# An encoder trunk on one core: wide products in the input projection, squares moved, two edits at the ends

## The chip, the core and the metric

The kernel runs on one core of a Trainium2 chip. The metric is the device time of one execution in microseconds, as the median of several runs. The engines are named as in the profile: PE (matrix products; PEld is its weight load), DVE (VectorE), ACT (ScalarE), POOL (GpSimd) and SP (it issues DMAs). Each has a queue of its own and works it off in order.

## The reference, cut to what matters

Two layers over 256 positions and 2048 channels, all in float32:

```python
hn = _rmsnorm(h, norm_g[i])
u = hn @ w_in[i]
a_val, a_glu, a_z, q, k, v, b_z = jnp.split(u, offs, axis=-1)
ya = _conformer_conv(a_val, a_glu, ...) * jax.nn.silu(a_z)   # GLU, 31-tap depthwise conv, LayerNorm, SiLU
yb = _window_attention(q, k, v, bias_band, sink[i]) * jax.nn.silu(b_z)
h = h + jnp.concatenate([ya, yb], axis=-1) @ w_out[i]
e = _rmsnorm(p[i] @ w_pe[i], pe_g[i])
h = h + e * jax.nn.sigmoid(h @ w_pg[i])
```

After the second layer a last RMSNorm is applied. The input projection has 5632 columns: 1024 each for the convolution's value, GLU and gate and for the query and the attention gate, 256 each for keys and values.

## The kernel before, in words

Everything is held transposed: 128 channels on the partitions, 256 positions along the row. To keep float32 accuracy on PE, each operand is split into a high and a low part (`hi`, rounded to PE's format, and `lo`, the rest), and a product of a weight tile w with an operand x is the sum of w_hi x_hi, w_hi x_lo and w_lo x_hi. `mm3` (L384) issues it in one of two ways. With a 256-column output it is three instructions of 256 columns into the same half of a PSUM bank (L391 to L393). With an output of three dimensions, a whole bank, it is one instruction of 512 columns, w_hi times x_hi and x_lo side by side (L388), and one of 256 columns, w_lo times x_hi, into the second half (L389). The two halves of the bank then have to be added: `merge` (L395) lets ACT copy the second half to SBUF and DVE add the first half to it. Before, only the gate of the embedding (the product with `w_pg`, tile `g`) is done in the wide way.

The weights stream in through 312 half tiles of 128 x 1024, 8 products each, in the order of `HALVES`: per layer 4 for the embedding's projection (`w_pe`), 32 for value and GLU (tile `ag`, 8 channel tiles), 4 for keys, 4 for values, 32 for attention gate and query in turn (tiles `zb` and `q`, pairs of tiles), 16 for the convolution gate (`za`), then 32 each for the output projection (`o`) and the embedding's gate (`g`). Working off one half is a step. At the start of step h the halves up to h + 4 are split (`get`, `ahead`, `split`, L159): ACT casts the high part (L163), DVE subtracts it from the weight (L166). There are five buffers of split weights. After each step `pump` (L198) is called once; it moves all side work on, which is written as generators: the generators in `side`, each by one `yield`, and then convolution taps from `conv_q`, at a rate per step that `RATES` sets by the place in the layer: one rate to the 56th half, one to the 80th, one behind. A convolution tile is one ACT instruction (L550) and 30 DVE taps (L557); two tiles run in turn. PE, DVE and ACT keep the order of the program as written, so this pump is the schedule.

The places that the change touches:

- `glu` (L564): after a value/GLU tile ACT takes the sigmoid of the GLU half from PSUM (L566) and DVE multiplies the value half with it (L567); then the tile joins the convolution queue. Value and GLU share one bank.
- The loop over `zb` and `q` (L668): `pair` fills one bank with two tiles of 256 columns. ACT takes the SiLU of the gate pair from PSUM (L671). Of the query pair ACT writes a negated, scaled high part (L677) and DVE the rest (L678); two generators of attention are queued, whose scores (tile `sc`, L626) come two steps later.
- The loop over `za` (L684) does the same as for the gate pair (L690).
- `embed` (L517): the generator for the RMSNorm of the embedding. Its squares are taken during the value/GLU stage, two tiles at a time, the square on ACT and the running sum on POOL (`square_acc`, L371); then a fold on DVE, a column of sums on PE, a power on POOL, and the row of factors. The factors are applied in the gate stage (L536), when `state["enorm"]` is set.
- The start (L274): x is loaded by four DMAs from ACT's queue, p and the first weights from SP's queue. PE begins with four products of zeros (L256).
- The end (L838): the last RMSNorm. A column of sums, power on POOL, a diagonal on DVE (L350), a product that spreads it over the partitions (tile `rfb`, L356). Ahead of that product PE is given 14 idle products (L842), each of two passes.

Of the kernel before, what the change touches and what calls it, by code (L numbers as in the profile page):

```python
# [10 lines left out]
F32 = mybir.dt.float32  # L11
F32R = mybir.dt.float32r
AF = mybir.ActivationFunctionType
# [4 lines left out]
P = 128  # L18
D = 2048
S = 256  # L20
# [105 lines left out]
def trunk_kernel(ctx: ExitStack, tc: tile.TileContext, xT, pT, wst, par, gain, relb, sinkp, onehot, out):  # L126
    nc = tc.nc
# [7 lines left out]
    wk = ctx.enter_context(tc.tile_pool(name="wk", bufs=2))  # L135
# [10 lines left out]
    def bank(name):  # L146
        return ps.tile([P, 2, S], F32, tag="ps", name=name)

    LD, LS = 3, NSPL - 1
    state = {"raw": -1, "spl": 3, "credit": 0.0}  # L150
# [42 lines left out]

    conv_q, side = [], []

    RATES = (3.3, 2.6, 3.3)

    def pump(taps=None):  # L198
        taps = RATES[(Cursor.h % NHALF > 4 + 32 + 8 + 12) + (Cursor.h % NHALF > 4 + 32 + 8 + 32 + 4)] if taps is None else taps
        state["credit"] += taps  # L200
        if ORD:
            sides()
        while state["credit"] >= 1 and conv_q:
            g = conv_q.pop(0)
            try:
                next(g)
                state["credit"] -= 1
                conv_q.insert(1, g)
            except StopIteration:
                pass  # L210
        if not conv_q:
            state["credit"] = 0.0
        if not ORD:
            sides()

    def sides():
        for g in list(side):
            try:
                next(g)
            except StopIteration:  # L220
                side.remove(g)
# [10 lines left out]
    def wait(n):  # L232
        for _ in range(n):
            yield
# [17 lines left out]
    zeros = wk.tile([P, S], F32, name="zeros", tag="sq", bufs=3)  # L252
# [10 lines left out]
    def load_half(c, x, n=1):  # L263

        if x == 0:
            raws[c] = wraw.tile([P, 2, HALF], F32, tag="raw", name=f"raw{c}")
        w = HALF // n
        for i in range(n):
            nc.sync.dma_start(raws[c][:, x, i * w:(i + 1) * w], wst[c, :, x * HALF + i * w:x * HALF + (i + 1) * w])

    def load_x(k):
        nc.scalar.dma_start(h[k // 8][:, k % 8:k % 8 + 4, :], xT[:, k:k + 4, :])

    h = halves(bigt("x"))  # L274
    pf = load_p(0)
    load_half(0, 0, 2)
    for k in range(0, KT, 4):
        load_x(k)
    load_half(0, 1)
# [38 lines left out]
    def bias_prep():  # L318
        nc.vector.tensor_scalar(nsink, sinkt, -1.0, None, ALU.mult)
        b = bank("fps").rearrange("p a b -> p (a b)")  # L320
        nc.tensor.matmul(b[0:NQ, 0:NREL], relt, oh, start=True, stop=True)
        fs = wk.tile([NQ, NREL], F32, name="fs", tag="sq", bufs=3)
        nc.vector.tensor_copy(fs, b[0:NQ, 0:NREL])
        nc.gpsimd.dma_start(fscr[:, 0:NREL], fs)
# [46 lines left out]
    def square_acc(acc, src, first, eng=None):  # L371

        if first:
            nc.scalar.activation(acc, src, AF.Square)
            return
        sq = wk.tile([P, 2, S], F32, name="sq", tag="sq", bufs=3)
        nc.scalar.activation(sq, src, AF.Square)
        (eng or nc.gpsimd).tensor_add(acc, acc, sq)
# [5 lines left out]
    def mm3(o, w, x, start, stop):  # L384
# [7 lines left out]
        nc.tensor.matmul(o, w[:, 0], x[:, 1], start=False, stop=False, skip_group_check=True)  # L392
        nc.tensor.matmul(o, w[:, 1], x[:, 0], start=False, stop=stop, skip_group_check=True)  # L393

    def merge(bs):  # L395

        t = wk.tile([P, 2, S], F32, name="hl", tag="ptt")[:, 0:len(bs), :]
        for x, b in enumerate(bs):
            nc.scalar.copy(t[:, x, :], b[:, 1, :])
            nc.vector.tensor_add(t[:, x, :], b[:, 0, :], t[:, x, :])  # L400
        return t

    class Cursor:
# [2 lines left out]
    def step(o, X, start, stop):  # L406

        steps([o], X, [start], stop)

    def steps(os, X, starts, stop):  # L410

        parts = []
        for _ in os:
            name, _, k0, nk = HALVES[Cursor.h % NHALF]
            parts.append(get(Cursor.h).rearrange("p t (k c) -> p t k c", k=nk))
            Cursor.h += 1
        for kk in range(nk):
            k = k0 + kk
            for o, w, start in zip(os, parts, starts):
                mm3(o, w[:, :, kk, :], X[k // 8][:, :, k % 8, :], start and kk == 0, stop and kk == nk - 1)  # L420
        for _ in os:
            pump()

    def pair(X, name):
        b = bank(name)
        for x in range(2):
            step(b[:, x, :], X, x == 0, False)
            step(b[:, x, :], X, False, True)
        return b

    def wide(X, name):

        b = bank(name)
        step(b, X, True, False)
        step(b, X, False, True)
        return b
# [6 lines left out]
    hacc = wk.tile([P, 2, S], F32, name="hacc", tag="hacc")  # L443
    for l in range(DEPTH):

        e = halves(bigt(f"e{l}"))
        eacc = wk.tile([P, 2, S], F32, name="eacc", tag="hacc")

        hg = []
        rbs, subs = [], []  # L450
# [21 lines left out]
        for q in range(4):  # L472
            n = Cursor.h
# [5 lines left out]
            for jj in range(0, 4, 2):  # L479
                j = 4 * q + jj  # L480
                b = bank("e")
# [32 lines left out]
        ahead(Cursor.h + 3)  # L514
        hsrc = xT if l == 0 else hscr

        def embed(l=l, eacc=eacc, e=e):  # L517

            if l == 0:
                yield from wait(8)  # L520
                bias_prep()
            for j in range(0, KT, 2):
                yield from wait(2)
                square_acc(eacc, e[j // 8][:, j % 8:j % 8 + 2, :], j == 0)
            yield from wait(6)
            es = fold(eacc)
            yield from wait(3)
            dg = rstd_col([es], D, f"re{l}")
            yield from wait(2)
            eb = rstd_row(dg, f"re{l}", "reb")  # L530
            yield from wait(50)
            while not state["enorm"]:
                yield
            for j in range(KT):
                d = e[j // 8][:, j % 8, :]
                nc.vector.scalar_tensor_tensor(d, d, pcol(l, PO_PE + j), eb, ALU.mult, ALU.mult)  # L536
                yield

        state["enorm"] = False
        engen = embed()  # L540
        side.append(engen)


        a, acc = halves(bigt(f"ac{l}"))
# [18 lines left out]

        def glu(t, b):  # L564
            u = wk.tile([P, S], F32, name=f"u{l}_{t}", tag="sg")
            nc.scalar.activation(u, b[:, 1, :], AF.Sigmoid)  # L566
            nc.vector.tensor_mul(a[:, t, :], b[:, 0, :], u)  # L567
            conv_q.append(conv(t))

        for ts in FIRST_TILES:  # L570
            bs = [bank(f"ag{l}_{t}") for t in ts]
            for n in range(2):
                for t, b in zip(ts, bs):
                    if len(ts) > 1:
                        steps([b[:, 0, :], b[:, 1, :]], hg, [n == 0, False], n == 1)
                        if n == 0:
                            operands(8 + 4 * t, 2)
                            subs.pop(0)()
                    else:
                        for x in range(2):  # L580
                            step(b[:, x, :], hg, n == 0 and x == 0, n == 1)
                    if n == 1:
                        glu(t, b)


        b = pair(hg, f"k{l}")
# [9 lines left out]
        for q in range(4):  # L596
            n = Cursor.h
# [12 lines left out]
        zb, za = halves(bigt(f"z{l}"))  # L610
# [56 lines left out]

        for i in range(0, 8, 2):  # L668

            b = pair(hg, f"zb{l}_{i}")  # L670
            nc.scalar.activation(zb[:, i:i + 2, :], b, AF.Silu)  # L671
            b = pair(hg, f"q{l}_{i}")

            qq = wk.tile([P, 2, 2, S], F32R, name="qq", tag="qq")
            for hh in range(2):
                r, o = rows_of[hh], rows_of[1 - hh]
                nc.scalar.mul(qq[r, :, hh, :], b[r], -(HD ** -0.5))  # L677
                nc.vector.scalar_tensor_tensor(qq[o, :, hh, :], b[r], -(HD ** -0.5), qq[r, :, hh, :].bitcast(F32),  # L678
                                               ALU.mult, ALU.subtract)
            for x in range(2):  # L680
                side.append(attention(i + x, qq[:, x], 4 * x))


        for t in range(0, NCT, 2):  # L684
            b = pair(hg, f"za{l}_{t}")
            if t == NCT - 2:
                finish(l)
                yb = bigt(f"yb{l}", F32R)
                nc.scalar.copy(yb[:, 0, 0:2, :], zb[:, 0:2, :])
            nc.scalar.activation(za[:, t:t + 2, :], b, AF.Silu)  # L690

        ya = bigt(f"ya{l}", F32R)

# [47 lines left out]
            step(ob[j // 2][:, j % 2, :], Y, j % 2 == 0, False)  # L741
        while lgen in side:
            pump(0)
        h1 = []

        def load_h(j):
# [27 lines left out]
        for j in range(NB_FIRST, KT, 2):  # L774
            b = bank(f"o{l}_{j}")
# [6 lines left out]
        hacc = wk.tile([P, 2, S], F32, name="hacc", tag="hacc")  # L782
# [43 lines left out]
        for j in range(KT - 2, KT):  # L826
            if last and j == KT - 1:
                b = bank(f"g{l}_{j}")[:, 0:1, :]
# [9 lines left out]
    dg = rstd_col(hparts, D, "rf")  # L838

    wb = bank("warm2")  # L840
    for _ in range(14):
        nc.tensor.matmul(wb[:, 0, 0:P], ones, ident, start=True, stop=True)  # L842
    rb = rstd_row(dg, "rf", copy=False)
    rbs = wk.tile([P, S], F32, name="rfrb", tag="rb", bufs=1)
# [86 lines left out]
```

## Time and profile before

| | |
|---|---|
| runs, median (lowest to highest) | 987.34 us (987.12 to 987.56) |
| profiled execution, its own time | 988.23 us |
| its span, first to last instruction | 986.5 us |
| mean granted PE clock | 0.995 |
| DVE, weight splits (L166) | 372.8 us busy, 306 instructions |
| ACT, weight casts (L163) | 316.2 us busy, 308 instructions |
| DVE, convolution taps (L557) | 480 instructions |

In rows of a timeline stand the start, the busy time, the engine, the line and operation, output and inputs by the program's names with partitions x elements, and in brackets the idle time of the engine before it with what ended it. Rows of busy time by stretch give the stretch, its length, the busy time and number of instructions of each engine asked for, the granted PE clock, and the share and rate of the DMAs. Rows of waits give who waited for whom: the total in us, how often, and the longest.

### The profile page before, as it was taken

What the parts mean: (1) busy time and instruction counts of PE and PEld (TensorE: products, weight loads), DVE (VectorE), ACT (ScalarE), POOL (GpSimd) and SP (SyncE); (2) the same over time, 40 slices, a digit from 0 to 9 for tenths busy, and PEclk for the clock granted to TensorE, in tenths of its full rate; (3) what the DMA queues carried; (4) which work ended last, traced back from release to release, by engine and by line L of the source; (5) the groups of instructions that cost most, each with busy time, mean ns of one, the idle gap of its engine ahead of it and who ended that gap; (6) DMA issues with size and microseconds to landing.
All of it is one profiled execution on the core that took longest, in us unless ns stands there. A gap on an engine that the chain in (4) does not pass through costs nothing.

```text
span 986.5 us, 18195 instructions
## 1 busy us (share of the span) xinstructions
PE 970.2 (98%) x7460; PEld 929.8 (94%) x7460; DVE 774.8 (79%) x1319; ACT 560.2 (57%) x861; POOL 86.8 (9%) x87
## 2 busy tenths in 40 slices
PE   8999999999999999999999999999999999999995
PEld 6999999999999999988899999999999999998885
DVE  3899989987787666687789998988887857567763
ACT  4654445778774554455566445468778555446551
POOL 0022001010000000011104200100100000000111
PEclk9999999999999999999999999999999999999997
DMA  7674546555544466446556555555453445654512
GB/s 283 245 247 171 190 147 218 174 186 171 178 153 179 144 234 232 171 171 228 199 184 233 176 208 173 175 183 204 155 178 144 171 166 179 232 201 145 216 70 85
DMA packets 29135, 182.49 MB, mean 185 GB/s; under 512 B 3723, under 2 KB 4284, under 8 KB 9212
## 3 DMA queue, kind: packets, MB, share of 16 engines
q1 hardware_dynamic: 24284, 165.17, 47.3%
q0 software_dynamic: 3472, 12.88, 4.4%
q10 hardware_dynamic: 1296, 3.28, 0.9%
q8 instruction: 58, 0.95, 0.4%
q14 instruction: 25, 0.20, 0.1%
HBM read 177.09 MB, written 4.23 MB: 184 GB/s over the span
## 4 chain that ended last, share of the span: by engine, by line
PE 97%; DVE 1%; DMA 1%; ACT 0%; issue 0%; POOL 0%; DVEq 0%; SPq 0%; ACTq 0%
PE g L388 12%; PE o L391 6%; PE o L392 6%; PE o L393 6%; PE ag L393 6%; PE ag L391 6%; PE ag L392 6%; PE g L389 6%; PE za L391 3%; PE zb L391 3%; PE q L391 3%; PE zb L392 3%; PE q L392 3%; PE za L392 3%; PE zb L393 3%; PE q L393 3%
## 5 line engine op out<-in xcount | busy, mean ns | idle before, releaser
L166 DVE TENSOR_TENSOR w<-raw,w 128x1024 fp32r<-128x1024 f32 x306 | 372.8, 1229 | 118.9 <-ACT w L163 115.9
L163 ACT CAST w<-raw 128x1024 fp32r<-128x1024 f32 x308 | 316.2, 1047 | 179.6 <-PE ag L393 45.3
L557 DVE SCALAR_TENSOR_TENSOR ac<-ac,pars 128x241 f32<-128x241 f32 (+11 forms) x480 | 218.3, 506 | 1.0
L388 PE MATMUL g<-h,w 128*128 128x512 f32 x496 | 175.3, 399 | 0.0
L393 PE MATMUL ag<-hg,w 128*128 128x256 f32 x512 | 145.1, 283 | 0.5 <-DVE w L166 0.5
L391 PE MATMUL ag<-hg,w 128*128 128x256 f32 x512 | 145.4, 284 | 0.0
L392 PE MATMUL ag<-hg,w 128*128 128x256 f32 x512 | 145.0, 283 | 0.1
L389 PE MATMUL g<-h,w 128*128 128x256 f32 x496 | 139.3, 281 | 0.0
L388 PEld LDWEIGHTS g<-h,w 128*128 128x128 f32 x496 | 93.2, 188 | 23.3
L391 PEld LDWEIGHTS ag<-hg,w 128*128 128x128 f32 x512 | 98.2, 192 | 0.9 <-ACT ac L550 0.8
L393 PEld LDWEIGHTS ag<-hg,w 128*128 128x128 f32 x512 | 98.2, 192 | 0.8 <-DVE w L166 0.7
L392 PEld LDWEIGHTS ag<-hg,w 128*128 128x128 f32 x512 | 98.2, 192 | 0.3 <-DVE hg L464 0.3
L389 PEld LDWEIGHTS g<-h,w 128*128 128x128 f32 x496 | 93.7, 189 | 0.0
L391 PE MATMUL za<-hg,w 128*128 128x256 f32 x256 | 73.7, 288 | 0.0
L391 PE MATMUL o<-yb,w 128*128 128x256 f32 x256 | 73.3, 286 | 0.0
L391 PE MATMUL q<-hg,w 128*128 128x256 f32 x256 | 73.3, 286 | 0.0
L391 PE MATMUL zb<-hg,w 128*128 128x256 f32 x256 | 73.1, 286 | 0.0
L392 PE MATMUL o<-yb,w 128*128 128x256 f32 x256 | 72.5, 283 | 0.0
L391 PE MATMUL o<-ya,w 128*128 128x256 f32 x256 | 72.4, 283 | 0.0
L392 PE MATMUL o<-ya,w 128*128 128x256 f32 x256 | 72.4, 283 | 0.0
L393 PE MATMUL o<-ya,w 128*128 128x256 f32 x256 | 72.4, 283 | 0.0
L393 PE MATMUL o<-yb,w 128*128 128x256 f32 x256 | 72.4, 283 | 0.0
(228 smaller groups left out, 2202.1 us busy)
## 6 DMA issues: line engine op xcount, KB each, us to landing
raw<-in_wst SPq DMA_DIRECT2D x153, 1024.0 KB, 4.9
bias<-fscr POOLq DMA_DIRECT2D x16, 384.0 KB, 3.8
raw<-in_wst SPq DMA_DIRECT2D x5, 512.0 KB, 9.1
x<-in_xT ACTq DMA_DIRECT2D x4, 512.0 KB, 7.5
hx<-in_xT POOLq DMA_DIRECT2D x8, 256.0 KB, 3.6
hscr<-e POOLq DMA_DIRECT2D x2, 1024.0 KB, 5.0
hx<-hscr POOLq DMA_DIRECT2D x8, 256.0 KB, 3.5
out_t<-og ACTq DMA_DIRECT2D x4, 256.0 KB, 3.0
```

What stands on the lines that cost most here:

```text
L163: nc.scalar.copy(hi, raw)
L166: nc.vector.tensor_sub(lo, raw, hi.bitcast(F32))
L388: nc.tensor.matmul(o, w[:, 0], x, start=start, stop=False, skip_group_check=True)
L389: nc.tensor.matmul(o[:, 1], w[:, 1], x[:, 0], start=False, stop=stop, skip_group_check=True)
L391: nc.tensor.matmul(o, w[:, 0], x[:, 0], start=start, stop=False, skip_group_check=True)
L392: nc.tensor.matmul(o, w[:, 0], x[:, 1], start=False, stop=False, skip_group_check=True)
L393: nc.tensor.matmul(o, w[:, 1], x[:, 0], start=False, stop=stop, skip_group_check=True)
L557: nc.vector.scalar_tensor_tensor(acc[:, t, lo_:hi_], a[:, t, lo_ + s:hi_ + s], w(k), acc[:, t, lo_:hi_], ALU.mult, ALU.add)
```

## The change

Gate, query, value, GLU and convolution gate tiles are done in the wide way, each tile in a bank of its own, followed by `merge1`, one tile's share of `merge`. Sigmoid, SiLU and the query's split then read the merged tile in SBUF. Keys and values stay as they are. The pump's first two rates change. The embedding's squares are summed on DVE, one pair of tiles per step, once `state["esum"]` is set, which is done in the output projection after the LayerNorm's generator has ended. At the start a Square of two columns of zeros stands ahead of x's DMAs in ACT's queue. At the end 3 idle products are left of 14.

```diff
-    RATES = (3.3, 2.6, 3.3)
+    RATES = (3.7, 2.3, 3.3)
...
     load_half(0, 0, 2)
+    first = wk.tile([P, 2], F32, name="first", tag="rv")
+    nc.scalar.activation(first, zeros[:, 0:2], AF.Square)
     for k in range(0, KT, 4):
         load_x(k)
...
+    def merge1(t, b):
+        nc.scalar.copy(t, b[:, 1, :])
+        nc.vector.tensor_add(t, b[:, 0, :], t)
...
-        def embed(l=l, eacc=eacc, e=e):
+        def embed(l=l, e=e):
             if l == 0:
                 yield from wait(8)
                 bias_prep()
+            while not state["esum"]:
+                yield
+            eacc = wk.tile([P, 2, S], F32, name="eacc", tag="hacc")
             for j in range(0, KT, 2):
-                yield from wait(2)
-                square_acc(eacc, e[j // 8][:, j % 8:j % 8 + 2, :], j == 0)
-            yield from wait(6)
+                square_acc(eacc, e[j // 8][:, j % 8:j % 8 + 2, :], j == 0, nc.vector)
+                yield
+            yield
             es = fold(eacc)
-            yield from wait(3)
+            yield
             dg = rstd_col([es], D, f"re{l}")
             yield from wait(2)
             eb = rstd_row(dg, f"re{l}", "reb")
-            yield from wait(50)
+            yield
...
             u = wk.tile([P, S], F32, name=f"u{l}_{t}", tag="sg")
-            nc.scalar.activation(u, b[:, 1, :], AF.Sigmoid)
-            nc.vector.tensor_mul(a[:, t, :], b[:, 0, :], u)
+            merge1(a[:, t, :], b[0])
+            merge1(u, b[1])
+            nc.scalar.activation(u, u, AF.Sigmoid)
+            nc.vector.tensor_mul(a[:, t, :], a[:, t, :], u)
             conv_q.append(conv(t))
...
-            bs = [bank(f"ag{l}_{t}") for t in ts]
+            bs = [[bank(f"ag{l}_{t}{x}") for x in range(2)] for t in ts]
...
-            b = pair(hg, f"zb{l}_{i}")
-            nc.scalar.activation(zb[:, i:i + 2, :], b, AF.Silu)
-            b = pair(hg, f"q{l}_{i}")
+            for x in range(2):
+                merge1(zb[:, i + x, :], wide(hg, f"zb{l}_{i + x}"))
+            nc.scalar.activation(zb[:, i:i + 2, :], zb[:, i:i + 2, :], AF.Silu)
+            b = wk.tile([P, 2, S], F32, name="qm", tag="u", bufs=3)
+            for x in range(2):
+                merge1(b[:, x, :], wide(hg, f"q{l}_{i + x}"))
...
-            b = pair(hg, f"za{l}_{t}")
+            for x in range(2):
+                merge1(za[:, t + x, :], wide(hg, f"za{l}_{t + x}"))
...
-            nc.scalar.activation(za[:, t:t + 2, :], b, AF.Silu)
+            nc.scalar.activation(za[:, t:t + 2, :], za[:, t:t + 2, :], AF.Silu)
...
         while lgen in side:
             pump(0)
+        state["esum"] = True
...
-    for _ in range(14):
+    for _ in range(3):
         nc.tensor.matmul(wb[:, 0, 0:P], ones, ident, start=True, stop=True)
```

More of the change, by code (lines that the diff above doesn't have):

```diff
@@ L398, in merge @@
         for x, b in enumerate(bs):
-            nc.scalar.copy(t[:, x, :], b[:, 1, :])
-            nc.vector.tensor_add(t[:, x, :], b[:, 0, :], t[:, x, :])
+            merge1(t[:, x, :], b)
         return t
@@ L446, in trunk_kernel @@
         e = halves(bigt(f"e{l}"))
-        eacc = wk.tile([P, 2, S], F32, name="eacc", tag="hacc")
         hg = []
@@ L537, in embed @@
                 yield
-        state["enorm"] = False
+        state["enorm"] = state["esum"] = False
         engen = embed()
@@ L574, in trunk_kernel @@
                     if len(ts) > 1:
-                        steps([b[:, 0, :], b[:, 1, :]], hg, [n == 0, False], n == 1)
+                        steps(b, hg, [n == 0] * 2, n == 1)
                         if n == 0:
@@ L580, in trunk_kernel @@
                         for x in range(2):
-                            step(b[:, x, :], hg, n == 0 and x == 0, n == 1)
+                            step(b[x], hg, n == 0, n == 1)
                     if n == 1:
```

## The prediction

> **What bounds the kernel now.** I read the page first, then the waits of TensorE (PE), then the busy time of VectorE (DVE) by stage, then timelines around each edited line.
>
> ```profile
> span 986.5 us, 18195 instructions
> PE 970.2 (98%) x7460; PEld 929.8 (94%) x7460; DVE 774.8 (79%) x1319; ACT 560.2 (57%) x861; POOL 86.8 (9%) x87
> ...
> PE 97%; DVE 1%; DMA 1%; ACT 0%; issue 0%; POOL 0%; DVEq 0%; SPq 0%; ACTq 0%
> ```
>
> PE is busy all through, and the chain that ended last is PE. The waits view has only four rows in which PE waits, 6.4 us in all with the two at the start; the other two:
>
> ```profile
> PE rfc L340 <- ACT sq L804: 1.6, 1, 1.6
> ...
> PE ag L393 <- DVE w L166: 0.5, 1, 0.5
> ```
>
> So a shorter PE program shortens the time, as long as the other engines deliver. Whether they do is read from the stages, because 79% is a mean. Layer 0, from the third value/GLU tile to the end of the first query pair, and then the gate tiles (us, DVE busy):
>
> ```profile
> 50.80:121.10 70.30, 69.63 (x111) 1.00 0.58 205
> 121.10:132.60 11.50, 9.55 (x20) 1.00 0.51 182
> 132.60:144.60 12.00, 9.54 (x20) 1.00 0.26 89
> 144.60:168.00 23.40, 23.33 (x41) 1.00 0.64 224
> ...
> 255.30:307.20 51.90, 43.48 (x91) 1.00 0.48 164
> ```
>
> Here is the second limit. In the first and fourth stretch DVE has almost no idle time (0.67 and 0.07 us). Over the first four it has 0.67 + 1.95 + 2.46 + 0.07 = 5.2 us. Work that the change puts on DVE before the first query pair meets this.
>
> **The products.** Starts of the same line, 11 narrow products apart, and of a wide line, 12 products apart:
>
> ```profile
> 100.03 0.28 PE L391 MATMUL ag<-hg,w 128*128 128x256 f32 x1
> ...
> 103.99 0.28 PE L391 MATMUL ag<-hg,w 128*128 128x256 f32 x1
> ```
>
> ```profile
> 409.61 0.40 PE L388 MATMUL g<-h,w 128*128 128x512 f32 x1
> ...
> 413.85 0.40 PE L388 MATMUL g<-h,w 128*128 128x512 f32 x1
> ```
>
> A product of three 256-column instructions takes 3.96/11 = 0.360 us, one of 512 and 256 columns 4.24/12 = 0.3533 us. The difference is 6.7 ns. By the code, both layers change 512 value/GLU products and 256 each for attention gate, query and convolution gate: 1280, so 8.5 us less PE time. A step (half a weight tile, 8 products, one call of the pump) goes from 2.880 to 2.827 us.
>
> The Trainium skill, "TensorE: Matmul & The Clock Gate", section "Back-to-back issue gap", gives a warm gap of columns/2.4 ns plus 2.5 ns. By that an estimate is 2.5 ns per product and 3.2 us in all, so the sum below would be 5.3 us higher; the rows show 0.120 us for 256 columns where it has 0.109, so the rows are used.
>
> **What it costs on DVE.** Prices, from DVE's timeline in the value/GLU stage, with one of the POOL additions:
>
> ```profile
> 66.01 2.69 DVE L557 SCALAR_TENSOR_TENSOR ac<-ac,pars 128x246 f32<-128x246 f32 x4
> ...
> 96.90 1.61 DVE L557 SCALAR_TENSOR_TENSOR ac<-ac,pars 128x242 f32<-128x242 f32 x4
> ...
> 101.55 0.41 DVE L567 TENSOR_TENSOR ac<-ag,u 128x256 f32<-128x256 f32 x1
> 101.88 1.21 DVE L166 TENSOR_TENSOR w<-raw,w 128x1024 fp32r<-128x1024 f32 x1
> 103.02 1.22 DVE L557 SCALAR_TENSOR_TENSOR ac<-ac,pars 128x241 f32<-128x241 f32 x3
> 104.16 1.21 DVE L166 TENSOR_TENSOR w<-raw,w 128x1024 fp32r<-128x1024 f32 x1
> ```
>
> ```profile
> 65.45 1.80 POOL L378 TENSOR_TENSOR eacc<-eacc,sq 128x512 f32<-128x512 f32 x1 [2.99 <-ACT sq L377]
> ```
>
> From start to start: a 256-column elementwise step 0.33, a weight split 1.14, a convolution tap 0.38. Four taps beside a POOL addition took 2.69 instead of 1.61: each such addition costs DVE 1.08 us, and the change takes seven away from this stage.
>
> A wide product leaves its two halves in PSUM, so every tile now needs an ACT copy and a DVE addition. Worse, ACT's sigmoid must wait for that addition, DVE's product for the sigmoid, and the next weight cast stands behind the sigmoid in ACT's queue, while DVE's split waits for that cast. This round trip is in the trace, at the end of the last stage:
>
> ```profile
> 963.47 0.42 DVE L400 TENSOR_TENSOR hl<-g,hl 128x256 f32<-128x256 f32 x1 [3.05 <-ACT hl L399]
> ...
> 963.99 0.42 ACT L796 ACTIVATE sg<-hl 128x256 f32<-128x256 f32 x1 [0.55 <-DVE hl L400]
> ...
> 964.44 0.42 DVE L798 TENSOR_TENSOR e<-e,sg 128x256 f32<-128x256 f32 x1 [0.21 <-ACT sg L796]
> ```
>
> ```profile
> 98.07 0.39 ACT L566 ACTIVATE u<-ag 128x256 f32<-128x256 f32 x1 [1.33 <-PE ag L393]
> 98.35 1.04 ACT L163 CAST w<-raw 128x1024 fp32r<-128x1024 f32 x1
> ```
>
> ```profile
> 156.52 0.60 ACT L671 ACTIVATE z<-zb 128x512 f32<-128x512 f32 x1 [0.52 <-PE zb L393]
> 157.01 1.04 ACT L163 CAST w<-raw 128x1024 fp32r<-128x1024 f32 x1
> ```
>
> Counted from the start of DVE's second addition: sigmoid at 0.52, product at 0.97 (DVE idle 0.64), cast at 0.52 + 0.28 = 0.80, its end at 1.84, so the split at 1.87 (idle another 0.57). Per value/GLU tile that is two additions 0.66 + 0.64 + 0.57 = 1.87 us of DVE. For a gate pair: two additions, then SiLU at 0.52, cast 0.49 later, split at 2.08 instead of 0.33: 0.66 + 1.75 = 2.4. For a query pair the negation on ACT (0.59 in the row below) now stands between DVE's addition and DVE's own part: 0.66 + 0.8 = 1.5. Before, ACT read PSUM itself, as soon as PE was done. A tile also holds two of the eight PSUM banks instead of one, until DVE's addition; with DVE four steps late that is four banks, so no bank is missing.
>
> Now the account, in each layer, to the first query pair. Added: the pump's rate goes from 3.3 to 3.7 for 40 steps, of which 30 in 31 are DVE taps: 0.4 x 40 x 30/31 = 15.5 taps, 5.9 us; seven tiles at 1.87, 13.1; one gate pair 2.4; the query pair 1.5. Together 22.9. Removed: seven POOL additions at 1.08, 7.6, and the embedding's fold, 0.3. Net 15.0 us. PE comes there 40 x 0.053 = 2.1 us earlier. DVE's idle 5.2 us takes up its part. What is left is lateness. How much of it PE bears:
>
> ```profile
> 167.72 0.28 PE L393 MATMUL q<-hg,w 128*128 128x256 f32 x1
> ```
>
> ```profile
> 168.04 0.59 ACT L677 ACTIVATE qq<-q 64x512 fp32r<-64x512 f32 x1 [1.83 <-PE q L393]
> ```
>
> ```profile
> 169.83 0.69 DVE L678 SCALAR_TENSOR_TENSOR qq<-q,qq 64x512 fp32r<-64x512 f32 x1
> 171.17 0.69 DVE L678 SCALAR_TENSOR_TENSOR qq<-q,qq 64x512 fp32r<-64x512 f32 x1 [0.66 <-ACT qq L677]
> ```
>
> ```profile
> 173.76 0.95 PE sc L626 x8
> ```
>
> The query products are through at 167.72 + 0.12. DVE comes to them 2.0 us later, needs 2.03 us to 171.86, and the scores, two steps behind, begin at 173.76, after 5.9 us. In the changed kernel DVE comes 2.0 + 15.0 - 5.2 + 2.1 = 13.9 us late, and may be late by 2 x 2.827 - 2.03 = 3.6. So PE loses 10.3 us in each layer, 20.6 in both. Part of it falls earlier, at the weight splits, which run four steps (11.3 us) ahead; that changes the place, not the sum. Behind that point DVE has slack again (8.4 us in the gate tiles, first fence of stages), the pump's rate falls to 2.3 there, and taps already done are not due again: I take nothing more, with 3 us per layer as the upper end. Lower end: if the idle waits inside the round trips (7 x 1.21 + 1.75 + 0.8 = 11.0) all found cover, DVE would be 2.9 late and PE would lose nothing. I stand near the upper end because in one queue in program order nothing lies between the addition and its user.
>
> **The embedding's squares** go to the output projection, onto ACT and DVE, where the row of the second half of that stage in layer 0 (PE, PEld, DVE, ACT, POOL) shows
>
> ```profile
> 350.00:401.80 51.80, 51.80 (x434) 51.80 (x433) 33.39 (x35) 23.82 (x27) 2.74 (x5) 1.00 0.66 229
> ```
>
> 18.4 us of DVE idle and 28 of ACT. Seven additions of twice the 0.33 step, a fold and the small row-norm steps are about 6 us: hidden, nothing. Without cover they would cost those 6 us per layer. The two small PE products of the row norm move along; nothing is saved by it. POOL's power step stands there behind loads of the residual, whose buffers are freed earlier in DVE's queue, so it holds up nobody for long.
>
> **The end.** Only idle products stand between DVE's diagonal and the last broadcast:
>
> ```profile
> 971.21 5.00 PE L842 MATMUL warm<-ident,ones 128*128 128x128 f32 x28
> ...
> 972.37 0.48 DVE L350 TENSOR_SCALAR rfdg<-ident,rfcol 128x128 f32<-128x128 f32 x2 [0.83 <-POOL rfcol L345]
> ...
> 976.04 0.60 PE L356 MATMUL rfb<-rfdg,ones 128*128 128x256 f32 x2
> ```
>
> ```profile
> 972.40:974.00 1.60, 1.60 (x10) 1.60 (x9) 0.46 (x2) 0.00 (x0) 0.00 (x0) 0.51 0.00 0
> ```
>
> 28 passes take 4.83 us, 0.173 each. Six end near 972.2, the diagonal at 972.85: the broadcast starts 3.15 us earlier. It then lies in the stretch with clock 0.51 and takes some 0.4 us longer. Gain 2.7.
>
> **The start.** A small Square is put before x's loads on ACT, so the function table is loaded first:
>
> ```profile
> 6.13 1.28 ACT L374 ACT_TABLE_LOAD   x1 [6.13 <-DMA x<-in_xT]
> ```
>
> ```profile
> 8.04 11.46 PE L487 MATMUL e<-p,raw 128*128 128x256 f32 x40 [3.07 <-DMA raw<-in_wst]
> ```
>
> The four issues of x move behind that Square; nothing else stands in ACT's queue there but squares that wait for x. x is asked for up to 2 us later, and p and the first weights, which PE awaits for 3.07 us, no longer share the transfer with it. Bounds: a gain of 3.07, or a loss of 0.7 if x becomes the bound (2 later, less the 1.28 of the table load). I take a gain of 2.0, nearer the wait that the row names.
>
> **Sum**, against the profiled execution, 988.2 us (span 986.5 and 1.7 around it): 988.2 - 8.5 - 2.7 - 2.0 + 20.6 = 995.6. The median of the runs shown is 987.3, 0.9 less; so 995 us.
>
> **Rivals.** Rival one, faster: ACT and DVE keep up, the round trips are covered, PE stays the bound. The time is 987.3 - 13.2 = 974. For it: with the round trips' waits left out, DVE's added work is 15.0 - 11.0 = 4.0 us, less than its 5.2 us of idle. Against it: no instruction stands in the queue that could fill the waits. It decides at 3.6 us of lateness at the first query pair. Chance 0.33, and another 0.03 for a loss of under 10 us that leaves a smaller gain.
>
> Rival two, no change: the loss in both layers is about 13 us, as large as the gains, which takes half of the waits to be covered: 987. Chance 0.06.
>
> Rival three, worse than forecast: DVE stays late through the second pair (3 us per layer), and PE's clock falls in the stall: after the 1.6 us wait for the last squares the row above has clock 0.51. One or two stretches of 3.4 us at half speed lose 1.7 to 3.4 us per layer. Together 7 to 13 us: 1002 to 1008. Chance 0.2. The Trainium skill, "TensorE: Matmul & The Clock Gate", section "Why this matters for your kernels", warns of idle gaps over some 3 us between bursts of products; a stall like the one forecast is of that kind, and the row's shorter wait already agrees.
>
> **Numbers.** The forecast, 988 to 1002, has 0.38. About 0.2%, 2 us, is what a measurement can tell here. Faster by more: 0.36; within: 0.06; slower by more: 0.38 + 0.2 = 0.58. The range runs from 973, to take in rival one, to 1006, leaving out the top of rival three and deeper gains. Both signs are in it.
>
> **What would show it.** Right: wide lines in the projection at 0.353 us per product; DVE near full in the value/GLU stage, with idle time put down to ACT's sigmoid and cast; new PE waits on DVE's split or on the query tiles, some 10 us per layer, the longest ahead of the first scores; the last broadcast near 3 us after the squares; none in the output projection. Wrong: PE waits still only at the start and the end, or DVE idle in the first stretch; then the round trips were covered. A clock under 1 in mid-span speaks for rival three.

## The result, and the profile after

| | before | after |
|---|---|---|
| median of four runs | 987.45 us (987.12 to 988.15) | 1003.56 us (1003.49 to 1003.60) |
| ratio, with its 95% interval | | 1.016 (1.0148 to 1.0173) |
| profiled execution, its own time | 988.23 us | 1003.6 us |
| span, mean granted PE clock | 986.5 us, 0.995 | 1001.8 us, 0.986 |

The changed kernel is 1.6% slower. The sign was forecast, with 7.7 us; it came to 16.1, more than twice that, a time that the prediction had left to its third rival. The head of the page after, the engines' busy times, and the shares of the chain that ended last:

```profile
span 1001.8 us, 15766 instructions
PE 965.1 (96%) x6158; PEld 859.1 (86%) x6158; DVE 796.0 (79%) x1413; ACT 578.1 (58%) x942; POOL 54.7 (5%) x73
...
PE 70%; DVE 23%; ACT 3%; issue 2%; DMA 1%; POOL 0%; SPq 0%; ACTq 0%; DVEq 0%
```

PE has 1302 instructions fewer and 5.1 us less busy time, and still the program is longer. The chain was 97% PE and 1% DVE; now 23% of it is DVE. DVE's mean share, 79%, is what it was. The waits of PE say where:

```profile
PE sc L637 <- DVE qq L692: 10.6, 2, 5.7
PE zb L392 <- DVE w L166: 4.2, 3, 2.0
...
PE v L395 <- DVE w L166: 1.8, 2, 0.9
...
PE k L396 <- DVE w L166: 1.4, 2, 0.7
...
PE ag L392 <- DVE w L166: 1.0, 2, 0.5
...
PE o L395 <- DVE yb L749: 0.6, 2, 0.3
```

The first row is the wait ahead of the first scores, once in each layer; the next four are waits for a weight split, the last is in the output projection. Before, only one of these rows was there (`ag`, 0.5 us). DVE by stage in layer 0, from the third value/GLU tile to behind the second query pair:

```profile
50.30:117.80 67.50, 61.40 (x115) 1.00 0.56 192
117.80:130.20 12.40, 11.40 (x23) 1.00 0.50 165
130.20:143.00 12.80, 12.73 (x25) 1.00 0.50 176
143.00:168.20 25.20, 23.40 (x42) 1.00 0.47 169
168.20:179.60 11.40, 10.67 (x23) 0.96 0.45 156
179.60:194.00 14.40, 13.63 (x31) 0.79 0.45 146
```

In the value/GLU stretch DVE is now idle for 6.1 us, where it was idle for 0.67, and that in a stage in which it is the engine that falls behind. That idle time lies inside the round trips. One of them, DVE and then ACT:

```profile
90.60 0.41 DVE L401 TENSOR_TENSOR ac<-ag,ac 128x256 f32<-128x256 f32 x1
90.94 0.41 DVE L401 TENSOR_TENSOR u<-ag,u 128x256 f32<-128x256 f32 x1
91.83 0.43 DVE L578 TENSOR_TENSOR ac<-ac,u 128x256 f32<-128x256 f32 x1 [0.48 <-ACT u L577]
92.77 1.23 DVE L166 TENSOR_TENSOR w<-raw,w 128x1024 fp32r<-128x1024 f32 x1 [0.51 <-ACT w L163]
```

```profile
91.38 0.42 ACT L577 ACTIVATE u<-u 128x256 f32<-128x256 f32 x1 [7.43 <-DVE u L401]
91.71 1.99 ACT L163 CAST w<-raw 128x1024 fp32r<-128x1024 f32 x2
```

From DVE's second addition (90.94) the product starts 0.89 us later and the split 1.83 us later; forecast were 0.97 and 1.87. ACT had waited 7.43 us for that addition, with two casts behind the sigmoid that do not use it.

Where the 15.3 us between the two spans lie, by the first start of each tile, in us:

| stage | layer 0 | layer 1 |
|---|---|---|
| start, to the first value/GLU product | -2.4 | |
| value/GLU, keys, values | +0.6 | +0.3 |
| gate and query pairs | +9.3 | +8.8 |
| gate tiles (`za`) | -1.0 | -1.1 |
| output projection | +1.7 | +1.7 |
| embedding's gate and the end | 0.0 | +0.1 - 2.7 |

In the first two stages the wide products alone take 3.4 us off each layer (512 of 6.7 ns), and two products of the row norm, 0.9 us, have left them (before, keys and values took 23.9 us in layer 0, where these products stand among them, and 23.0 in layer 1). So 14.2 us are lost there in layer 0 and 13.4 in layer 1.

### The profile page after: what moved, and what is told of

Same layout as the page of the kernel before. It is cut to its first block, busy times and chain, and to the rows that moved or that the text cites. A ratio compares the mean times of both kernels' runs of the same rounds, so it can differ in the third digit from the quotient of the medians.

```text
span 1001.8 us, 15766 instructions
## 1 busy us (share of the span) xinstructions
PE 965.1 (96%) x6158; PEld 859.1 (86%) x6158; DVE 796.0 (79%) x1413; ACT 578.1 (58%) x942; POOL 54.7 (5%) x73
## 4 chain that ended last, share of the span: by engine, by line
PE 70%; DVE 23%; ACT 3%; issue 2%; DMA 1%; POOL 0%; SPq 0%; ACTq 0%; DVEq 0%
PE g L391 12%; DVE w L166 9%; DVE ac L566 9%; PE o L395 6%; PE za L391 6%; PE o L394 6%; PE o L396 6%; PE g L392 6%; PE q L391 4%; PE zb L391 4%; PE ag L391 4%; PE za L392 3%; PE q L392 2%; PE ag L392 2%; ACT w L163 2%; PE zb L392 2%
## 5 line engine op out<-in xcount | busy, mean ns | idle before, releaser
L163 ACT CAST w<-raw 128x1024 fp32r<-128x1024 f32 x308 | 311.0, 1045 | 71.8 <-PE g L392 22.0
L566 DVE SCALAR_TENSOR_TENSOR ac<-ac,pars 128x241 f32<-128x241 f32 (+11 forms) x480 | 203.2, 474 | 1.1
L391 PE MATMUL ag<-hg,w 128*128 128x512 f32 x512 | 181.2, 398 | 0.2 <-DVE hg L470 0.2
L392 PE MATMUL ag<-hg,w 128*128 128x256 f32 x512 | 144.5, 282 | 1.3 <-DVE w L166 1.0
L391 PEld LDWEIGHTS ag<-hg,w 128*128 128x128 f32 x512 | 96.2, 188 | 24.3 <-issue 0.9
L392 PEld LDWEIGHTS ag<-hg,w 128*128 128x128 f32 x512 | 96.8, 189 | 3.5 <-DVE w L166 3.3
L391 PE MATMUL zb<-hg,w 128*128 128x512 f32 x256 | 95.4, 411 | 0.0
L391 PE MATMUL za<-hg,w 128*128 128x512 f32 x256 | 92.1, 402 | 0.0
L391 PE MATMUL q<-hg,w 128*128 128x512 f32 x256 | 91.7, 400 | 0.0
L392 PE MATMUL za<-hg,w 128*128 128x256 f32 x256 | 71.6, 280 | 0.0
```

Of the source, the lines that this page charges most:

```text
L163: nc.scalar.copy(hi, raw)
L391: nc.tensor.matmul(o, w[:, 0], x, start=start, stop=False, skip_group_check=True)
L392: nc.tensor.matmul(o[:, 1], w[:, 1], x[:, 0], start=False, stop=stop, skip_group_check=True)
L566: nc.vector.scalar_tensor_tensor(acc[:, t, lo_:hi_], a[:, t, lo_ + s:hi_ + s], w(k), acc[:, t, lo_:hi_], ALU.mult, ALU.add)
```

## The experiments

**Theory.** DVE, not PE, sets the time from the value/GLU stage to the second query pair, because it stands idle in the round trips: addition on DVE, ACT's function, its user on DVE, the next cast on ACT, the next split on DVE. The same instructions in another order should then give back all of the loss. **Rivals.** DVE simply has too much work there (taps, additions); the pump's rate is to blame; or PE's clock, which falls in the stall, makes the larger part of what the forecast missed.

"Before" and "after" are the two kernels compared; every other kernel is one of them with the edit shown. All medians, and ratios to the kernel before with their 95% intervals:

| kernel | us | ratio |
|---|---|---|
| before with the two edits at the ends | 983.92 | 0.9962 (0.9948 to 0.9976) |
| after with the old rates | 989.10 | 1.0014 (1.0005 to 1.0023) |
| after with narrow value/GLU | 989.33 | 1.0019 (1.0010 to 1.0029) |
| after, value/GLU's round trip opened | 985.69 | 0.998 (0.9971 to 0.9989) |
| after, sigmoid and product behind the next cast | 988.09 | 1.0006 (0.9996 to 1.0015) |
| after, gate's and query's round trips opened | 994.47 | 1.0065 (1.0048 to 1.0082) |
| after, all of them opened | 975.17 | 0.9875 (0.9860 to 0.9890) |
| the same with the old rates | 975.38 | 0.9874 (0.9856 to 0.9892) |
| after with the squares back in the value/GLU stage | 1019.09 | 1.0322 (1.0306 to 1.0338) |
| after with idle products in the stall | 1003.13 | 1.0157 (1.0142 to 1.0172) |

### The ends alone

The kernel before with the Square ahead of x's loads and 3 idle products at the end.

```diff
+    first = wk.tile([P, 2], F32, name="first", tag="rv")
+    nc.scalar.activation(first, zeros[:, 0:2], AF.Square)
...
-    for _ in range(14):
+    for _ in range(3):
```

> The kernel before with only the two edits at its ends: the Square ahead of x's loads and 3 idle products for 14. Theory (a late DVE costs the changed kernel its time, the ends are gains): 987.4 - 2.3 - 2.7 = 982.4. Rival (the ends are worth nothing or cost something, and the losses lie elsewhere): 987 or more.

983.92 us: 3.65 less than before by medians. In its trace the first value/GLU product starts at 23.9 us, not 26.2, and the end is 2.7 shorter; by the spans it is 4.9, of which 0.7 is that the profiled execution before lay above its median and 0.6 that the one here lay below its own. So both ends are gains, as they were taken for, though the median is 1.5 us above the 982.4 expected. In the changed kernel the first weights still come last (a wait of 1.74 us, where it was 3.07), and the last broadcast waits for DVE:

```profile
6.64 1.97 PE L493 MATMUL e<-p,raw 128*128 128x256 f32 x8 [1.74 <-DMA raw<-in_wst]
```

```profile
989.18 0.92 PE L858 MATMUL warm<-ident,ones 128*128 128x128 f32 x6
...
990.98 1.01 PE L359 MATMUL rfb<-rfdg,ones 128*128 128x256 f32 x2 [0.88 <-DVE rfdg L353]
```

The six idle passes end before the diagonal is there, and PE waits 0.88 us: there are no idle products left to save on the path.

### The pump's rates put back

```diff
-    RATES = (3.7, 2.3, 3.3)
+    RATES = (3.3, 2.6, 3.3)
```

> The changed kernel with the pump's old rates (3.3, 2.6, 3.3). Theory: 5.9 us per layer of taps move behind the first query pair, PE's wait there shrinks by as much and the slow clock may go with it: 1003.6 - 2 x 5.9 = 992, to 986 if the clock holds. Rival (the lateness is not from the taps, or is only paid later): 1001 or more.

989.10, so 14.5 us less than after, for 15.5 taps per layer up to the first query pair, 5.9 us of DVE, 11.8 in both. The waits ahead of the first scores are smaller and still there:

```profile
PE sc L637 <- DVE qq L692: 8.3, 2, 4.3
```

More than the price of the taps came back, as from a stage in which DVE is the bound. So with the round trips closed the rate decides over 14.5 of the 16.1 us. It does so only together with the idle time: two kernels below, with the round trips opened, differ in the rate alone and take the same time.

### Value and GLU narrow again

```diff
-            merge1(a[:, t, :], b[0])
-            merge1(u, b[1])
-            nc.scalar.activation(u, u, AF.Sigmoid)
-            nc.vector.tensor_mul(a[:, t, :], a[:, t, :], u)
+            nc.scalar.activation(u, b[:, 1, :], AF.Sigmoid)
+            nc.vector.tensor_mul(a[:, t, :], b[:, 0, :], u)
```

(and both in one bank again)

> The changed kernel with value and GLU back at three 256-column products, sigmoid and product straight from PSUM; the rest stays wide. Theory: 13.1 of the 22.9 us that were put on DVE per layer go, DVE reaches the first query pair within its 3.6 us, PE's waits of about 9 us per layer and the slow clock behind them vanish: the ends' 982.4 less 768 x 6.7 ns = 5.1, so 977 (to 984 if the other round trips still bite). Rival (the waits come from the tap rate and the gate and query merges): above 992.

989.33: the expectation missed by 12 us. Without the seven round trips of the value/GLU stage DVE is still late at the first scores, under the higher rate and the wide gate and query pairs:

```profile
PE sc L635 <- DVE qq L690: 5.0, 3, 2.4
```

So the account of DVE's lateness is short by some us: without the seven tiles it has 15.0 - 13.1 = 1.9 us of net work, which the 5.2 us of idle time should have taken up. Its trace shows that it was not taken up: over the same four stretches (49.0 to 165.5 us here) DVE is idle for 3.0 + 0.4 + 2.2 + 1.7 = 7.4 us. Of these, 1.64 lie in the gate pair's round trip, and 2.07 are a wait for the keys' high part that is in before as well, with 2.3. The stretch behind PE's wait (PE, PEld, DVE, ACT, POOL, clock):

```profile
174.00:177.40 3.40, 3.40 (x14) 3.02 (x13) 3.40 (x6) 2.08 (x3) 0.00 (x0) 0.51 0.02 5
```

After a wait of only 2.4 us PE ran 3.4 us at half clock.

### Value and GLU's round trip opened

The sigmoid is issued after the next step's cast and split, the product one step later:

```diff
-            nc.scalar.activation(u, u, AF.Sigmoid)
-            nc.vector.tensor_mul(a[:, t, :], a[:, t, :], u)
-            conv_q.append(conv(t))
+            def ready():
+                nc.scalar.activation(u, u, AF.Sigmoid)
+                yield
+                nc.vector.tensor_mul(a[:, t, :], a[:, t, :], u)
+                conv_q.append(conv(t))
+            side.append(ready())
```

> The changed kernel with the same instructions in another order: the sigmoid of a value/GLU tile is issued after the next step's weight cast, the product one step later, so that DVE and ACT no longer stand still between them. If the idle waits of the round trip are the cause (1.21 of 1.87 us per tile, 8.5 us per layer): about 980 (974 to 988). Rival (the added DVE work itself is too much): above 995.

985.69, 17.9 us less than after, with the same instructions on every engine; it is in the range expected, 5.7 above its 980. Seven tiles of 0.64 + 0.57 us in two layers are 16.9. This is the theory's main point, and it speaks against too much work by itself: the work is unchanged. What is left of the waits is that of the query pair:

```profile
PE sc L640 <- DVE qq L695: 6.4, 3, 3.8
```

### The two waits of one round trip

To tell the wait for the sigmoid (0.64) from that for the cast (0.57), sigmoid and product were issued together, both behind the next step's cast and split:

```diff
+            def ready():
+                nc.scalar.activation(u, u, AF.Sigmoid)
+                nc.vector.tensor_mul(a[:, t, :], a[:, t, :], u)
+                conv_q.append(conv(t))
+                return
+                yield
+            side.append(ready())
```

> The changed kernel with the sigmoid and the product of a value/GLU tile issued together behind the next step's weight cast and split: DVE still waits for the sigmoid, the split no longer for a cast behind the sigmoid. It tells the two waits of the round trip apart. Theory: the 0.51 us wait at the split goes, seven tiles in each layer, and PE's wait at the first scores falls by 3.6 us: 1003.6 - 7 = 997, a little lower with the second pair. Rival (the sigmoid's wait only grows by as much, or only removing both helps): 1002 or more.

988.09: the expectation missed by 9 us, because the experiment does not separate the two. DVE's queue has the split between the addition and the product now, and the split is longer than the wait:

```profile
78.51 0.42 DVE L401 TENSOR_TENSOR ac<-ag,ac 128x256 f32<-128x256 f32 x1
78.84 0.42 DVE L401 TENSOR_TENSOR u<-ag,u 128x256 f32<-128x256 f32 x1
79.17 1.22 DVE L166 TENSOR_TENSOR w<-raw,w 128x1024 fp32r<-128x1024 f32 x1
80.31 0.42 DVE L579 TENSOR_TENSOR ac<-ac,u 128x256 f32<-128x256 f32 x1
```

No idle time stands in any of these rows. One split, 1.14 us, covers the whole round trip; a full step of distance gives 2.4 us more. How the 1.21 us divide by their effect stays open. The start of this kernel is that of after, but in its profiled execution PE waits 3.7 us for the first weights, not 1.74, and value/GLU begins at 25.9 us, not 23.8: the gain at the start is not there in every execution.

### Gate's and query's round trips opened

SiLU goes behind the next cast (for the gate pairs and for all but the last `za` pair), and the negation on ACT and DVE's part of the query's split lie a step apart, with the scores two steps later:

```diff
-            nc.scalar.activation(zb[:, i:i + 2, :], zb[:, i:i + 2, :], AF.Silu)
+            later(nc.scalar.activation, zb[:, i:i + 2, :], zb[:, i:i + 2, :], AF.Silu)
...
+            def negate(i=i, b=b, qq=qq):
+                ...
+                yield
+                ...
+            side.append(negate())
...
-                side.append(attention(i + x, qq[:, x], 4 * x))
+                side.append(attention(i + x, qq[:, x], 2 + 4 * x))
```

> The changed kernel with the value/GLU tiles as they are, but the round trips of the gate and query pairs opened as in all_later. Theory: at the first query pair DVE is 1.75 + 0.8 us earlier and its allowance some 0.9 us larger, so the wait there falls from 5.7 and 4.9 to about 2 us, and the 3 us per layer that are lost behind it go: 1003.6 - 6.9 - 6 = 991 (987 to 994). Rival (the value/GLU round trips are the whole cause, since glu_later alone gained 17.9): 999 or more.

994.47, 9.1 us less than after and just above the 987 to 994 expected. What the later scores do of this and what the opened round trips do was not separated. The waits ahead of the scores are down from 10.6 us to 0.5, and 0.7 that is put down to a cast; those for the splits stay:

```profile
PE zb L392 <- DVE w L166: 4.0, 2, 2.0
...
PE sc L637 <- ACT w L163: 0.7, 2, 0.4
...
PE sc L637 <- DVE qq L696: 0.5, 2, 0.2
```

### All of them opened, at either rate

Both edits together, and the same with the old rates.

> All round trips opened: the value/GLU product as in glu_later, the SiLU of the gate pairs one step later, the query's negation on ACT in one step and DVE's part in the next, scores two steps later. The changed kernel's rates. Theory: DVE's allowance at the first query pair grows from 3.6 to some 4.5 us and its idle waits go, so the wait for the first scores (6.4 us in two layers in glu_later) and the slow clock go too: 985.7 - 6.4 - 3.4 = 976. Rival (what is left is DVE's work, or a new wait of the later attention at the end of the stage): 983 or more.

> The same with the old rates (3.3, 2.6, 3.3). Theory: DVE is 5.9 us earlier at the first query pair, no wait is left there: 974 to 977. If taps are then missing at the end, a wait for the mean of the LayerNorm shows, and the time is above all_later's.

975.17 and 975.38. Against after that is 28.4 us; the two edits alone gave 17.9 and 9.1, 27.0 in sum. This kernel beats both, and it is 8.75 us below the kernel with the two edits at the ends: as PE bounds both, this is about the worth of the wide products, forecast at 8.5. The largest of PE's waits, and the largest between the first value/GLU product and the gate tiles:

```profile
PE e L493 <- DMA raw<-in_wst: 1.7, 1, 1.7
PE rfc L343 <- ACT sq L831: 1.6, 1, 1.6
...
PE ag L392 <- DVE w L166: 0.5, 1, 0.5
PE pt L667 <- ACT s L661: 0.4, 1, 0.4
```

The first two are the start and the end; no wait for the query is left. DVE in the first of the six stretches shown above, and their sum:

```profile
50.30:117.80 67.50, 66.96 (x126) 1.00 0.57 202
...
sum 143.70, DVE 142.43; mean DVE 23.74
```

DVE does 126 instructions in the time in which it did 115, and over the six stretches it is idle for 1.3 us, not 10.5 (143.7 less the 133.2 of the rows after). It is full, and PE hardly waits: the work fits, just.

### The squares back

After with the embedding's squares where they were before, on ACT and POOL in the value/GLU stage (the `embed` of before).

> The changed kernel with the embedding's squares back in the value/GLU stage, summed on POOL. Theory (each POOL addition takes 1.08 us from DVE, seven per layer, and DVE is the bound there): 1003.6 + 2 x 7.6 = 1019. Rival (these additions fall into DVE's idle waits, or the squares cost as much in the output projection): 1000 to 1006.

1019.09, 15.5 us more than after: if all of it is put on the POOL additions (14 in both layers), 1.11 each, forecast at 1.08. In a stage that DVE bounds, moving them away was worth all of it. PE's waits for DVE in this kernel:

```profile
PE ag L392 <- DVE w L166: 9.9, 13, 1.4
PE sc L635 <- DVE qq L690: 7.9, 3, 4.3
PE re1b L359 <- DVE re1dg L353: 5.3, 1, 5.3
PE re0b L359 <- DVE re0dg L353: 4.7, 1, 4.7
```

The last two rows, 10.0 us, are new: the row norm's own product stands in this stage again, and DVE, late by then, has not made its operand. PE meets DVE's lateness wherever it next needs something of it.

The output projection takes 94.6 us here, 95.4 in after and 93.7 before. So the moved row norm is 0.8 us of after's 1.7. The other 0.9 stay with the squares gone; 0.3 of that is the wait for `yb`, and the rest was not traced.

### Idle products in the stall

Does the clock cost the 9 us that the rows of waits do not explain (27.6 lost in the first two stages of both layers, 18.5 in the waits)? After with 24 idle products of 128 columns ahead of the first scores in each layer:

```diff
+            if i == 0:
+                wb = bank("warm3")
+                for _ in range(24):
+                    nc.tensor.matmul(wb[:, 0, 0:P], ones, ident, start=True, stop=True)
```

> The changed kernel with 24 idle products of 128 columns given to PE in each layer ahead of the first scores, where it waits 5.7 and 4.9 us for the query tiles anyway. Theory (the wait drops PE's clock, and the slow stretches behind it cost about 3.4 us in each layer): no slow stretch there, 1003.6 - 6.8 = 997. Rival (the slow stretches cost nothing, since DVE is late anyway): 1003 or more.

1003.13, 0.4 us less than after; the mean clock rose from 0.986 to 0.993. The stretch behind the first scores, first of after, then of this kernel (PE, PEld, DVE, ACT, POOL, clock):

```profile
179.60:194.00 14.40, 14.38 (x68) 12.47 (x69) 13.63 (x31) 9.57 (x18) 0.72 (x1) 0.79 0.45 146
```

```profile
179.90:194.00 14.10, 13.87 (x82) 12.12 (x83) 13.61 (x31) 9.29 (x18) 0.72 (x1) 1.00 0.44 137
```

PE gets 14 instructions further in it. DVE does the same 31 instructions in the same time, and PE then waits instead, for attention's ACT and DVE work:

```profile
197.67 0.44 PE L668 MATMUL pt<-ident,s 128*128 128x128 f32 x2 [1.01 <-ACT s L662]
```

At the start of the second query pair this kernel is 2.1 us ahead (187.08 against 189.16), at the start of the third gate pair 0.3 (201.97 against 202.24). Ahead of the scores and behind them, the clock's fall is a mark of the stall; the time is DVE's. Elsewhere it was not held: in layer 1 the clock falls for some 3.4 us behind a 2.0 us wait for a weight split, in after (632.8 to 636.2 us, 0.50) and in this kernel (632.6 to 636.0, 0.57).

## Why the prediction's size was wrong, and what of it held

**Right: the mechanism.** The round trip was read from a row of the last stage at 1.87 us from addition to split; 1.83 was measured. For the gate pair 2.08 was taken, and DVE shows

```profile
164.98 0.42 DVE L401 TENSOR_TENSOR z<-zb,z 128x256 f32<-128x256 f32 x1
...
167.04 1.22 DVE L166 TENSOR_TENSOR w<-raw,w 128x1024 fp32r<-128x1024 f32 x1 [1.64 <-ACT w L163]
```

2.06. At the first query pair PE's waits, splits and scores together, were forecast at 10.3 us per layer. In layer 0 they are 10.0 (5.7 + 2.2 + 1.0 + 0.9 + 0.7, less the 0.5 that stood there before), in layer 1 8.5 (4.9 + 2.0 + 0.9 + 0.7), and the longest is the one ahead of the first scores (DVE's part first, then PE's):

```profile
177.77 0.41 DVE L401 TENSOR_TENSOR qm<-q,qm 128x256 f32<-128x256 f32 x1
178.88 1.40 DVE L692 SCALAR_TENSOR_TENSOR qq<-qm,qq 64x512 fp32r<-64x512 f32 x2 [0.70 <-ACT qq L691]
```

```profile
179.62 0.58 PE L637 MATMUL sc<-keys0h,qq 128*128 128x256 f32 x1 [5.70 <-DVE qq L692]
```

The judgement that nothing in the queue covers the waits held, and rival one's condition, that they are covered, was made true by hand: it gave 975.17 where that rival had 974.

**Right: the small terms.** Products -8.75 (forecast -8.5), the end -2.7 (-2.7), the start -2.4 (-2.0), a POOL addition 1.11 us (1.08). By the Trainium skill's gap formula ("TensorE: Matmul & The Clock Gate", section "Back-to-back issue gap"), which it gives for single products, the prediction's estimate for the products was 3.2 us; the runs side with the rows of the trace.

**Wrong: the step "I take nothing more" behind the first query pair.** Of the 14.2 and 13.4 us that are lost from value/GLU to the gate tiles, 2.6 and 2.1 come there, 4.7 in all, where the sum had nothing. From the first scores to the gate tiles PE takes 79.5 and 79.0 us; before it took 78.1 in both layers, and the 176 wide products among them should have saved 1.2. PE hardly waits there, but at first, here in layer 0, it runs at half clock:

```profile
180.00:182.00 2.00, 2.00 (x9) 1.78 (x9) 1.69 (x3) 2.00 (x4) 0.00 (x0) 0.50 0.22 86
182.00:184.00 2.00, 2.00 (x7) 1.71 (x7) 2.00 (x5) 0.73 (x1) 0.00 (x0) 0.50 0.00 0
```

With the clock held (the last experiment) this stretch still takes 79.0 us in layer 0: 0.5 of the 2.6 are gained, and PE is idle for 1.6. The slack that the forecast leaned on lies in the gate tiles, 80 us further on. Between are three more gate and query pairs with the same round trips; up to 194 us DVE is busy for 13.63 of 14.40, and only behind that does it show idle time again (busy for 11.94 of 14.00 to 208 us). The first wait takes away the lateness beyond the 3.6 us allowed, not its cause. The prediction's own upper end for this, 3 us per layer, held. It had priced rival three's two parts, lateness and clock, as adding up; behind the first scores they are the same microseconds.

**Too small: the loss up to the first scores.** It is 11.6 and 11.3 us, forecast at 10.3, and more than the rows of waits add up to (10.0 and 8.5). From start to start each of these waits costs 0.1 to 0.2 us more than the idle time in its row: ahead of the keys' first waiting product 0.99 us lie between two starts that are otherwise 0.12 apart, so 0.87 are lost, for a row of 0.7. In layer 1 the half clock behind the 2.0 us wait takes 1.7 us more, half of its 3.4. Since DVE decides when the first scores can start, PE would likely have waited these out there; that was not tried.

**The 8.6 us by terms.** Against the forecast: +4.7 behind the first scores, +2.3 ahead of them, +1.7 in the output projection beside the moved products (which leave one stage and come back in the other), -0.8 at the start and in the gate tiles, +0.1 in the embedding's gate, and +0.9 that was taken off because the profiled execution before lay above its median, while that of after lay on it. That is 8.9; the other 0.3 is the forecast's own rounding up.

**The squares in the output projection** were taken as hidden, and DVE's part is: PE does not wait for them. The two row-norm products that move along were taken as nothing for the whole program; they are 0.8 to 0.9 us out of one stage and into another. The output projection is 1.7 us longer in each layer all the same: 0.9 of it stays with the squares gone.

## What to carry to other kernels

Before work is moved onto an engine that is full in that stage, count the round trips it makes through a second in-order queue, and put independent work (here the next split, 1.14 us) between an operation and the user of its result: the same instructions in another order were 28.4 us apart. A higher rate of taps, worth nothing once the round trips were opened, cost 14 us beside the closed ones. Follow lateness to every later consumer up to the first stage that shows idle time; the first wait does not end it. A fallen clock behind a stall need not be what costs the time: hold it once with idle work and see whether the feeder is any faster.

## What the runs showed of the hardware

PE's granted clock fell to about half for 3.4 us behind waits as short as 1.6 us: before behind the 1.6 us wait for the last squares (972.4 to 975.8 us, clock 0.51 and then 0.50), in layer 1 of after behind one of 2.0 (632.8 to 636.2, 0.50), in the kernel with narrow value/GLU behind one of 2.4 (0.51). Behind an equal wait of 2.0 us at the same place in layer 0 of after it stayed at 1.00 (146 to 152 us). So the length of the wait alone does not decide. After the 5.7 us wait the clock was low for twice as long:

```profile
179.62:186.42 6.80, 6.80 (x25) 0.56 0.27 70
```

What else decides was not tried. The Trainium skill, "TensorE: Matmul & The Clock Gate", section "Why this matters for your kernels", has gaps over some 3 us as what to avoid; the three waits of 1.6 to 2.4 us here were shorter.

An addition of 128 x 512 on POOL cost a full DVE 1.11 us, if the whole difference of the two kernels is put on the 14 additions; four taps beside one in the profile of before had shown 1.08.
